# The last preparation ahead of the block products of Up, and the last gate's steps behind them, in another order

## The chip, the cores and the metric

The kernel runs on one core of a Trainium2 chip. The metric is the device time of one execution in microseconds (us), lower is better. Three runs of the kernel before gave 693.24, 691.15 and 691.52 us; the median is 691.52.

Engines are named as in the profile: PE is TensorE's matrix multiplication, PEld its loading of weights, DVE is VectorE, ACT ScalarE, POOL GpSimd, SP SyncE, which issues most DMAs (SPq is its queue). Each engine works off its own instructions in the order in which they are written; engines wait for one another by semaphores.

## The reference

One layer of a decoder, batch 1, 512 positions, width 1024, in f32. The change lies in its second half:

```python
mod = cs @ w_ada[l] + b_ada[l]                     # cs = silu(c)
sh1, sc1, gt1, sh2, sc2, gt2 = [m[:, None, :] for m in jnp.split(mod, 6, axis=-1)]
...
h2 = rmsnorm(x, norm2_g[l]) * (1.0 + sc2) + sh2
u = causal_dwconv(h2 @ w_up[l], conv_w[l], conv_b[l])   # w_up: 1024 x 5632, taps of width 3
a, v = jnp.split(u, 2, axis=-1)                         # 2816 columns each
x = x + gt2 * ((jax.nn.silu(a) * v) @ w_down[l])
```

What comes ahead of it (the projection, linear recurrence and sparse attention) is not touched.

## The kernel before

Every f32 operand of a matrix product is split into a high part (a cast by ScalarE, L150) and a low part (source minus high part, by VectorE, L151). `mm3` makes three matmuls of each product: high times high (L154), high times low (L155), low times high (L156). In the rows the parts of weights are called `whi`, `wlo` (or `wg` for both, in another pool), those of `h2` `h2h`, `h2l`. Thus weights must be loaded, cast and subtracted before the third matmul that uses them; for a down tile, where weights are the moving side's partner, `whi` serves the first and `wlo` the second matmul.

The Up product is computed in transposed form, 128 columns of `w_up` by 512 positions a tile. There are 44 such column blocks, and they run in this order:

- Sixteen plain tiles, `up_mm(st, ...)`, of 24 matmuls of 512 columns each: st 0 to 7 (`HEAD`, four column blocks of `a` and the same four of `v`) ahead, and st 8 to 15 (`BODY`) behind.
- Between them seven groups, `x_group(n)`, `n` from 0 to 6. A group makes the four column blocks `j`, `j+11` of `a` and of `v`: two by plain products (`v_mm`, weights `v1` and `v2`), two by a 2x2 block product with fewer multiplications, in which sums of weight blocks meet sums of blocks of `h2`. Sums of weights are three VectorE operations, `prepare_sums` (`t` or `t12` from `raw`); `prepare_plain` splits the blocks `b`, `prepare_rest` makes `t4` and splits the blocks `c`, `prepare_other` splits `v1`; within the group follow the splits of `t12`, of `x4` and of `v2`. Group `n` prepares group `n+1`; group 0 is prepared in the last tiles of the head. The sums of `h2` are made by POOL (`ar`, L1911 and the lines ahead of it) and split, one a tile, by `x_sum` in st 3 to 6 (rows `sx`).

Behind each tile come its `taps` (one ACT and two DVE operations, rows `y`) and its `gate` (Silu on ACT for `a`; three or four POOL operations, rows `ga` and `gb`, for `v`). They are written two tiles behind the tile. What is still open when the groups begin is held in a list and called at three places in a group.

Beside these runs the last gate, `gt2`: it is a matrix product with one row only, so `w_ada`'s slice is scaled by ScalarE and added up by POOL. `last_begin` clears `gt2` (a POOL memset), loads the row of `b_ada` and the first piece; `last_fetch` loads a piece (`aw`), `last_add` scales and adds one and fetches the next, sixteen in all, eight for each half `q`. `last_end(gt2, q)` splits the sum of a half into `rhi` and `rlo`, adds it up over the partitions by two matmuls with a matrix of ones (`ps<-rhi,onesr`, `ps<-rlo,onesr`: the spread), and copies `ps` back to `gt2`.

Loads of weights stand in a fixed list, `loads`; `take` issues them two or three ahead into `raw`, of two buffers; each third load of the groups goes into a lent buffer, `aw`, of one. A further chain of DMAs, `weight_sums(tick)`, sums blocks of `w_down` in memory, by SP (plain copies) and POOL (accumulating DMAs); `put_by` stores parts of the gated tiles in memory and splits others (rows `as`). Behind st 15 begins the down product (`dn`), whose weights come by `dn_load(u)` and are split by `dn_split(u)`.

Of the kernel before, what the change touches and what calls it, by code (L numbers as in the profile page):

```python
# [9 lines left out]
F32 = mybir.dt.float32  # L10
# [9 lines left out]
P = 128  # L20
# [89 lines left out]
def hybrid_layer_kernel(ctx: ExitStack, tc: tile.TileContext, d: dict, out: bass.AP, dbg=None):  # L110
# [14 lines left out]
    def nm(s):  # L125
        uid[0] += 1
        return f"{s}_{uid[0]}"
# [82 lines left out]

    loads += [up_load(f) for f in HEAD]
    first_x = len(loads)
    loads += [x_load(j, h) for j in XS for h in range(2)]
    last_x = len(loads)
# [3 lines left out]
    def issue():  # L218
        if len(issued) < len(loads):
            name, shape, pieces = loads[len(issued)]  # L220
            n = len(issued) - first_x
            if 0 <= n < 2 * len(XS) and n % 3 == 0:
                raw = wp.tile([P] + shape, F32, tag="aw", name=nm("raw"), bufs=1)
            else:
                raw = wp.tile([P] + shape, F32, tag="raw", name=nm("raw"))
            for sl, src in pieces:
                sp.dma_start(raw[sl], src)
            issued.append(raw)
# [1283 lines left out]

    def last_end(res, q):
        assert not last_raw
        acc = res[:, q * 512:(q + 1) * 512]
        hi, lo = (TMP([P, 512], F32R, tag=t) for t in ("rhi", "rlo"))
        split(hi, lo, acc)
        ps = PS()
        pe.matmul(ps, onesr, hi, start=True, stop=False)
        pe.matmul(ps, onesr, lo, start=False, stop=True)  # L1520
        sc.copy(acc, ps)

# [193 lines left out]
    us = {}  # L1716
# [53 lines left out]
    def gate(s, f):  # L1770
# [14 lines left out]
        else:  # L1785
# [3 lines left out]
            gp.tensor_tensor(a[:, 3], a[:, 0], b[:, 3], ALU.subtract)  # L1789

    def up_post(st):
        f, s = NF[st // 2], st % 2
        taps(us.pop(st), s, f)
        gate(s, f)

# [29 lines left out]
    def dn_load(u):  # L1825
        ph, v = divmod(u, NU)
        j = PAIRS[v]
        if u < 2:
            t = wp.tile([P, 2, 2, 512], F32, tag="raw", name=nm("raw"))
            r0, r1 = t[:, 0], t[:, 1]  # L1830
        else:
            r0, r1 = (G([2, 512], s="wd") for _ in range(2))
# [72 lines left out]
    up_mm(2, hi_half)  # L1905
    up_post(0)
    A = {(r, q): araw.pop((q, r)) for r in range(2) for q in range(2)}
    gp.tensor_tensor(A[1, 1], A[1, 0], A[1, 1], ALU.subtract)
# [65 lines left out]
    def x_group(n):  # L1974
# [14 lines left out]
        v_mm(V[0], p["v1"], range(4))  # L1989
        held.pop(0)()  # L1990
        beside()
        x_mm(X, half(p["t12"], 1), ops[2], False)
# [28 lines left out]
        if more:  # L2021
            prepare_other(n + 1)
        else:
            piece()
        del prep[n]

# [21 lines left out]
    for st in range(3, NH):  # L2048
        beside()
        up_mm(st, full)  # L2050
        up_post(st - 2)
        x_sum()
        if st == 3:
            last_begin(5, gt2)
        else:
            last_add(5, gt2)
        if st == NH - 3:
            prepare_sums(0)
        elif st == NH - 2:
            prepare_plain(0)  # L2060
        elif st == NH - 1:
            prepare_other(0)
            prepare_rest(0)
    held += [lambda: up_post(NH - 2), lambda: up_post(NH - 1), lambda: None]
    for n in range(len(XS)):
        x_group(n)
    SX.clear()
    for st in range(NH, nst):
        beside()
        if st == nst - 1:  # L2070
            dn_load(0)
            dn_load(1)
        up_mm(st, full)
        if held:
            for f in held:
                f()
            held.clear()
        elif st > NH + 1:
            up_post(st - 2)
        if st < NH + 5:  # L2080
            last_add(5, gt2)
        elif st < NH + 7:
            last_end(gt2, st - NH - 5)
    dn_split(0)
# [141 lines left out]
```

## Time and profile before

| | |
|---|---|
| median of 3 runs | 691.52 us |
| the profiled execution | 696.19 us, span 694.4 us |
| mean granted clock of TensorE | 0.988 |
| PE busy | 669.5 us, 96% of the span, 4400 matmuls |
| DVE, ACT, POOL busy | 552.9, 382.8, 180.7 us |
| st 3 begins | 343.21 us |
| group 0, group 1 begin | 373.51, 403.48 us |
| st 8 begins | 530.68 us |
| first down tile begins | 583.03 us |

Times within the execution count from the start of its span. In a row of the timeline stand the start, the duration, the engine, the line, the operation, what is written and read (`out<-in`), the shapes, and in brackets how long the engine stood idle just before and what released it.

### The profile page before, as it was taken

The page shows a single profiled execution, that of the slowest core. Times are in us where ns is not written, and L with a number is a line of the kernel's source. Part 1 is how long each engine was busy: PE and PEld are TensorE (multiplying, and loading weights), DVE is VectorE, ACT ScalarE, POOL GpSimd, SP SyncE. Part 2 cuts the span into 40 slices and gives each one's busy share as a digit, 9 for nine tenths or more (in the row PEclk, how much of TensorE's full clock was granted, in tenths as well). Part 3 has the DMA queues.
Part 4 walks back from the last instruction along what each step waited for, and adds up shares of the span by engine and source line. Part 5 has one row for each costly group of instructions (what it writes and reads, how often), then busy time and mean ns, then how long its engine had stood idle before and what let it go on. Part 6 is the DMA issues. An engine that isn't in the chain of part 4 may idle for free.

```text
span 694.4 us, 11710 instructions
## 1 busy us (share of the span) xinstructions
PE 669.5 (96%) x4400; PEld 562.1 (81%) x4400; DVE 552.9 (80%) x1038; ACT 382.8 (55%) x713; POOL 180.7 (26%) x172
## 2 busy tenths in 40 slices
PE   8999999999999999999997899999999988999996
PEld 4678898688888888888985798898988766888885
DVE  4788988978899878788568578988886877676997
ACT  4756437747777875346554454554554645465551
POOL 1006120000010101100656235664445864100000
PEclk9999999999999999999999899999999999999999
DMA  8936364566214135145356899999997736786672
GB/s 335 405 128 201 96 219 125 194 194 209 92 33 155 60 120 184 62 129 182 118 165 184 227 238 244 255 281 266 265 234 197 213 93 217 271 347 243 201 286 91
DMA packets 101885, 134.67 MB, mean 194 GB/s; under 512 B 6507, under 2 KB 67780, under 8 KB 101829
## 3 DMA queue, kind: packets, MB, share of 16 engines
q1 hardware_dynamic: 96885, 121.28, 51.5%
q0 software_dynamic: 4512, 11.54, 9.9%
q10 hardware_dynamic: 432, 1.12, 0.4%
q8 instruction: 34, 0.56, 0.3%
q14 instruction: 22, 0.18, 0.1%
HBM read 125.39 MB, written 31.60 MB: 226 GB/s over the span
## 4 chain that ended last, share of the span: by engine, by line
PE 69%; DVE 15%; ACT 7%; issue 3%; DMA 3%; POOL 1%; SPq 0%; ACTq 0%; DVEq 0%; POOLq 0%
PE u L154 5%; PE u L155 5%; PE u L156 5%; PE dn L155 5%; PE dn L156 5%; PE dn L154 5%; DVE wlo L151 4%; PE uf L156 4%; PE uf L155 3%; PE uf L154 3%; PE accq L679 3%; PE oh L154 2%; PE oh L156 2%; PE oh L155 2%; PE oT L1148 2%
## 5 line engine op out<-in xcount | busy, mean ns | idle before, releaser
L151 DVE TENSOR_TENSOR wlo<-raw,whi 128x1024 fp32r<-128x1024 f32 (+1 forms) x53 | 68.4, 1293 | 40.4 <-ACT whi L150 40.3
L156 PE MATMUL u<-h2h,wlo 128*128 128x512 f32 (+1 forms) x248 | 94.2, 380 | 3.1 <-DVE wlo L151 3.1
L154 PE MATMUL u<-h2h,whi 128*128 128x512 f32 (+1 forms) x248 | 94.4, 380 | 0.0
L155 PE MATMUL u<-h2l,whi 128*128 128x512 f32 (+1 forms) x248 | 94.0, 379 | 0.0
L150 ACT CAST whi<-raw 128x1024 fp32r<-128x1024 f32 (+1 forms) x53 | 53.9, 1018 | 17.3 <-PE u L155 6.9
L156 PEld LDWEIGHTS u<-h2h,wlo 128*128 128x128 f32 x248 | 47.0, 190 | 13.9 <-DVE wlo L151 5.2
L155 PEld LDWEIGHTS u<-h2l,whi 128*128 128x128 f32 x248 | 47.3, 191 | 7.9
L154 PEld LDWEIGHTS u<-h2h,whi 128*128 128x128 f32 x248 | 47.3, 191 | 7.7
L150 ACT CAST whi<-wd 128x1024 fp32r<-128x1024 f32 x20 | 21.1, 1055 | 39.8 <-PE dn L156 34.4
L371 POOL TENSOR_TENSOR hrs<-hrs,mhalf 128x4 f32<-128x4 f32 (+2 forms) x16 | 18.6, 1174 | 90.7 <-DVE hrs L370 88.6
L1086 ACT ACTIVATE pt<-pt,mx 128x128 f32<-128x128 f32 (+3 forms) x64 | 36.0, 564 | 9.2 <-DVE mx L1070 8.1
L154 PE MATMUL pT<-hT,whi 128*128 128x512 f32 x96 | 38.3, 399 | 0.0
L151 DVE TENSOR_TENSOR wlo<-wd,whi 128x1024 fp32r<-128x1024 f32 x20 | 25.5, 1275 | 15.4 <-ACT whi L150 15.3
L155 PE MATMUL pT<-hT,whi 128*128 128x512 f32 x96 | 37.6, 391 | 0.0
L156 PE MATMUL pT<-hT,wlo 128*128 128x512 f32 x96 | 37.5, 391 | 0.0
L155 PE MATMUL dn<-wlo,as 128*128 128x512 f32 x88 | 34.3, 390 | 0.1
L156 PE MATMUL dn<-whi,as 128*128 128x512 f32 x88 | 34.2, 389 | 0.0
L154 PE MATMUL dn<-whi,as 128*128 128x512 f32 x88 | 34.2, 389 | 0.0
L1126 ACT COPY pT<-F 128x512 f32<-128x512 f32 (+2 forms) x52 | 25.8, 499 | 13.5 <-PE F L1119 13.4
L1787 POOL TENSOR_TENSOR ga<-y,y 128x256 f32<-128x256 f32 x11 | 13.7, 1244 | 73.7 <-ACT y L1773 58.9
L1070 DVE CUSTOM_DVE_ANT_0 pt<-S,cmask 128x128 f32<-128x128 f32 (+3 forms) x64 | 29.7, 485 | 2.2 <-PE S L1066 2.0
L1773 ACT ACTIVATE y<-y 128x512 f32<-128x512 f32 x22 | 13.9, 633 | 30.8 <-DVE y L1767 30.8
(409 smaller groups left out, 2046.3 us busy)
## 6 DMA issues: line engine op xcount, KB each, us to landing
raw<-in_w_up SPq DMA_DIRECT2D x44, 512.0 KB, 6.8
aw<-in_w_ada SPq DMA_DIRECT2D x24, 512.0 KB, 3.9
ada<-in_ada_first SPq DMA_DIRECT2D x16, 512.0 KB, 7.9
raw<-in_w_in SPq DMA_DIRECT2D x7, 1024.0 KB, 5.5
wt<-in_w_down POOLq DMA_DIRECT2D x11, 512.0 KB, 9.0
wd<-in_w_down SPq DMA_DIRECT2D x11, 512.0 KB, 4.3
wt<-in_w_down SPq DMA_DIRECT2D x10, 512.0 KB, 5.2
wt<-in_w_down POOLq DMA_DIRECT2D x5, 1024.0 KB, 11.1
```

The lines of the kernel that those rows point to most:

```text
L150: sc.copy(hi, src)
L151: (eng or ve).tensor_tensor(lo, src, f32(hi), ALU.subtract)
L154: pe.matmul(o, ah, bh, start=start, stop=False, skip_group_check=True)
L155: pe.matmul(o, ah, bl, start=False, stop=False, skip_group_check=True)
L156: pe.matmul(o, al, bh, start=False, stop=stop, skip_group_check=True)
L371: gp.tensor_tensor(o, o, mhalf[:, 0:n], ALU.pow)
L679: pe.matmul(accq[i], h[:, e, i * P:(i + 1) * P], w[:, f], start=(k + e + f == 0), stop=(e == 1 and k == KT - 1), skip_group_check=True)
L1070: ve.tensor_tensor_reduce(pt[:, e * W:(e + 1) * W], ps[:, e * W:(e + 1) * W], cmask[:, 512 - W:512], -1.0, 1e30, ALU.add, ALU.min, mx[:, e ...
L1086: sc.activation(pt[:, sl], pt[:, sl], AF.Exp, bias=mx[:, e:e + 1], scale=-1.0, accum_out=su[:, h % 2, e:e + 1])
L1126: sc.copy(pT, ps[:, 0:n * P])
L1148: pe.matmul(oTs[i][r:r + 64, h // 2], VV[:, j, b, g], src[:, q * P:(q + 1) * P], start=(h == 0 and b == 0 and j == 0), stop=False, skip_gr ...
L1773: sc.activation(y, y, AF.Silu)
```

## The change

Five things are written elsewhere; no operation is added or left out.

1. The first load of group 0 (`ux2`) stands ahead of the head's last weight load and goes into the lent buffer; every third of the groups' loads after it does, as before.
2. Group 0's preparation is spread over st 4 to 7: sums, plain, rest, other. Before, the sums stood at st 5, plain at st 6, other and rest at st 7. In st 3 to 7 the taps come first, then `x_sum` and the preparation, then the gate.
3. `last_begin` stands ahead of POOL's four sums of `h2`. There is no `last_add` in st 4 to 7; groups 5 and 6 have a second one, st 8 has two, and st 9 to 13 one each.
4. `last_end` is cut in two. `last_split` of the first half stands at st 9 and `last_spread` at st 10; those of the second half at st 14 and st 15.
5. `dn_load(0)` stands at st 13, into the lent buffer, in place of st 15.

```diff
-    loads += [up_load(f) for f in HEAD]
+    x_loads = [x_load(j, h) for j in XS for h in range(2)]
+    loads += [*[up_load(f) for f in HEAD[:-1]], x_loads[0], up_load(HEAD[-1])]
     first_x = len(loads)
-    loads += [x_load(j, h) for j in XS for h in range(2)]
+    loads += x_loads[1:]
+    lent = {id(x) for x in x_loads[::3]}
...
-    def last_end(res, q):
+    def last_split(res, q):
         hi, lo = (TMP([P, 512], F32R, tag=t) for t in ("rhi", "rlo"))
-        split(hi, lo, acc)
+        split(hi, lo, res[:, q * 512:(q + 1) * 512])
+        last_parts.extend((hi, lo))
+
+    def last_spread(res, q):
         ps = PS()
-        pe.matmul(ps, onesr, hi, start=True, stop=False)
-        pe.matmul(ps, onesr, lo, start=False, stop=True)
-        sc.copy(acc, ps)
+        for n in range(2):
+            pe.matmul(ps, onesr, last_parts.pop(0), start=(n == 0), stop=(n == 1))
+        sc.copy(res[:, q * 512:(q + 1) * 512], ps)
...
-            t = wp.tile([P, 2, 2, 512], F32, tag="raw", name=nm("raw"))
+            t = wp.tile([P, 2, 2, 512], F32, tag=("raw" if u else "aw"), name=nm("raw"), bufs=2 if u else 1)
...
     up_post(0)
+    last_begin(5, gt2)
     A = {(r, q): araw.pop((q, r)) for r in range(2) for q in range(2)}
...
+        if n > 4:
+            last_add(5, gt2)
         beside()
...
             piece()
+            last_fetch(5)
...
     for st in range(3, NH):
         beside()
         up_mm(st, full)
-        up_post(st - 2)
+        post_taps(st - 2)
         x_sum()
-        if st == 3:
-            last_begin(5, gt2)
-        else:
-            last_add(5, gt2)
-        if st == NH - 3:
+        if st == NH - 4:
             prepare_sums(0)
-        elif st == NH - 2:
+        elif st == NH - 3:
             prepare_plain(0)
+        elif st == NH - 2:
+            prepare_rest(0)
         elif st == NH - 1:
             prepare_other(0)
-            prepare_rest(0)
-    held += [lambda: up_post(NH - 2), lambda: up_post(NH - 1), lambda: None]
+        post_gate(st - 2)
+
+    def between():
+        post_gate(NH - 2)
+        post_taps(NH - 1)
+
+    held += [lambda: post_taps(NH - 2), between, lambda: post_gate(NH - 1)]
...
     for st in range(NH, nst):
         beside()
-        if st == nst - 1:
+        if st == nst - 3:
             dn_load(0)
+        elif st == nst - 1:
             dn_load(1)
         up_mm(st, full)
...
-        if st < NH + 5:
+        for _ in range(2 if st == NH else st < NH + 6):
             last_add(5, gt2)
-        elif st < NH + 7:
-            last_end(gt2, st - NH - 5)
+        if st in (NH + 2, nst - 1):
+            last_spread(gt2, st == nst - 1)
+        if st in (NH + 1, nst - 2):
+            last_split(gt2, st == nst - 2)
     dn_split(0)
```

What this does to the engines' queues shows at three places. The first is VectorE's queue from st 4 to the last preparation ahead of group 0. Numbers behind names tell buffers apart; `wlo_792` before and `wlo_793` now are the low part of st 6's weights, `wlo_802` and `wlo_801` of st 7's, `t12_799` and `t12_789` the first group's sums. Before:

```order
L151 TENSOR_TENSOR sx_787_4345<-ar_754_4026,sx_786_4344 128x1024
L151 TENSOR_TENSOR wlo_792_4358<-raw_773_4262,whi_791_4357 128x1024
L1766 SCALAR_TENSOR_TENSOR y_793_4385<-u_772_4261,cv_3498,y_793_4385 128x511
L1767 SCALAR_TENSOR_TENSOR y_793_4385<-u_772_4261,cv_3498,y_793_4385 128x510
L151 TENSOR_TENSOR sx_795_4394<-ar_727_3879,sx_794_4393 128x1024
L1943 TENSOR_TENSOR t12_799_4407<-raw_790_4354 128x512
L1944 TENSOR_TENSOR raw_790_4354<-raw_790_4354 128x512
L1945 TENSOR_TENSOR t12_799_4407<-raw_790_4354 128x512
L151 TENSOR_TENSOR wlo_802_4413<-raw_773_4262,whi_801_4412 128x1024
L1766 SCALAR_TENSOR_TENSOR y_803_4440<-u_782_4310,cv_3498,y_803_4440 128x511
L1767 SCALAR_TENSOR_TENSOR y_803_4440<-u_782_4310,cv_3498,y_803_4440 128x510
L151 TENSOR_TENSOR sx_805_4446<-ar_728_3880,sx_804_4445 128x1024
```

Now:

```order
L151 TENSOR_TENSOR sx_787_4344<-ar_754_4026,sx_786_4343 128x1024
L1954 TENSOR_TENSOR t12_789_4350<-raw_774_4266 128x512
L1955 TENSOR_TENSOR raw_774_4266<-raw_774_4266 128x512
L1956 TENSOR_TENSOR t12_789_4350<-raw_774_4266 128x512
L151 TENSOR_TENSOR wlo_793_4361<-raw_788_4347,whi_792_4360 128x1024
L1771 SCALAR_TENSOR_TENSOR y_794_4388<-u_773_4265,cv_3498,y_794_4388 128x511
L1772 SCALAR_TENSOR_TENSOR y_794_4388<-u_773_4265,cv_3498,y_794_4388 128x510
L151 TENSOR_TENSOR sx_796_4393<-ar_727_3879,sx_795_4392 128x1024
L151 TENSOR_TENSOR wg_798_4397<-raw_774_4266,wg_797_4396 128x1024
L151 TENSOR_TENSOR wlo_801_4406<-raw_788_4347,whi_800_4405 128x1024
L1771 SCALAR_TENSOR_TENSOR y_802_4433<-u_782_4310,cv_3498,y_802_4433 128x511
L1772 SCALAR_TENSOR_TENSOR y_802_4433<-u_782_4310,cv_3498,y_802_4433 128x510
```

The three sums stand ahead of st 6's low part in place of behind it, and the first split of the group (`wg`) ahead of st 7's.

The second is SyncE's queue from `last_begin` and the first loads of `wt0` on (`raw<-in_w_up` are weights of Up, `gt2<-in_b_ada` the row of `last_begin`, `aw` pieces of the gate, `wt0` the sums of `w_down` in memory). Before:

```order
L1737 DMA wt0_3798<-in_w_down 128x2x512
L1738 DMA wt0_3798<-in_w_down 128x2x512
L227 DMA raw_773_4262<-in_w_up 128x8x128 x2
L1503 DMA gt2_3810<-in_b_ada 1x1024
L1498 DMA aw_781_4308<-in_w_ada 128x512
L1498 DMA aw_788_4350<-in_w_ada 128x512
L227 DMA raw_790_4354<-in_w_up 128x8x128 x2
L1498 DMA aw_796_4399<-in_w_ada 128x512
L227 DMA raw_797_4401<-in_w_up 128x8x128 x2
L227 DMA raw_798_4404<-in_w_up 128x8x128 x2
L1498 DMA aw_806_4451<-in_w_ada 128x512
L1742 DMA wt0_3798<-wt0_3798 128x2x512
```

Now:

```order
L1504 DMA gt2_3810<-in_b_ada 1x1024
L1499 DMA aw_772_4257<-in_w_ada 128x512
L1742 DMA wt0_3798<-in_w_down 128x2x512
L1743 DMA wt0_3798<-in_w_down 128x2x512
L228 DMA raw_774_4266<-in_w_up 128x8x128 x2
L228 DMA raw_788_4347<-in_w_up 128x8x128 x2
L228 DMA raw_791_4357<-in_w_up 128x8x128 x2
L1747 DMA wt0_3798<-wt0_3798 128x2x512
L228 DMA raw_810_4478<-in_w_up 128x8x128 x2
```

The row of `b_ada` and one piece stand ahead of `wt0`'s loads; the other pieces are gone from here, and the copy `wt0<-wt0` stood behind four weight loads and stands behind three, ahead of the fourth (`raw_798` before, `raw_810` now, the first for group 1).

The third is ScalarE's queue from st 15 into the down product (`gt2<-ps` copies a spread half, `whi_1082` and `wg_1084` are the high parts of the first down tile). Before:

```order
L1765 ACTIVATE y_1072_6318<-u_1054_6199,cv_3498 128x512
L1773 ACTIVATE y_1072_6318<-y_1072_6318 128x512
L150 CAST rhi_1073_6323<-gt2_3810 128x512
L1521 COPY gt2_3810<-ps_1075_6327 128x512
L1765 ACTIVATE y_1079_6365<-u_1060_6240,cv_3498 128x512
L150 CAST whi_1082_6374<-raw_1076_6332 128x1024
L150 CAST wg_1084_6378<-raw_1076_6332 128x1024
L1765 ACTIVATE y_1086_6382<-u_1069_6289,cv_3498 128x512
```

Now:

```order
L1770 ACTIVATE y_1073_6322<-u_1057_6205,cv_3498 128x512
L1778 ACTIVATE y_1073_6322<-y_1073_6322 128x512
L150 CAST rhi_1074_6327<-gt2_3810 128x512
L1770 ACTIVATE y_1078_6361<-u_1064_6250,cv_3498 128x512
L1526 COPY gt2_3810<-ps_1081_6370 128x512
L150 CAST whi_1082_6374<-raw_1063_6246 128x1024
L150 CAST wg_1084_6378<-raw_1063_6246 128x1024
L1770 ACTIVATE y_1086_6382<-u_1070_6293,cv_3498 128x512
```

The copy of the second half stood ahead of the taps of tile 13 and of the down tile's casts; it now stands behind these taps, directly ahead of the casts. On TensorE the two matmuls that it waits for stood behind st 14's, and now stand behind st 15's.

More of the change, by code (lines that the diff above doesn't have):

```diff
@@ L220, in issue @@
             name, shape, pieces = loads[len(issued)]
-            n = len(issued) - first_x
-            if 0 <= n < 2 * len(XS) and n % 3 == 0:
+            if id(loads[len(issued)]) in lent:
                 raw = wp.tile([P] + shape, F32, tag="aw", name=nm("raw"), bufs=1)
@@ L1511, in last_add @@
         last_fetch(s)
-    def last_end(res, q):
-        assert not last_raw
-        acc = res[:, q * 512:(q + 1) * 512]
+    last_parts = []
+    def last_split(res, q):
+        assert all(raw[1] > q for raw in last_raw)
         hi, lo = (TMP([P, 512], F32R, tag=t) for t in ("rhi", "rlo"))
-        split(hi, lo, acc)
+        split(hi, lo, res[:, q * 512:(q + 1) * 512])
+        last_parts.extend((hi, lo))
+    def last_spread(res, q):
         ps = PS()
-        pe.matmul(ps, onesr, hi, start=True, stop=False)
-        pe.matmul(ps, onesr, lo, start=False, stop=True)
-        sc.copy(acc, ps)
+        for n in range(2):
+            pe.matmul(ps, onesr, last_parts.pop(0), start=(n == 0), stop=(n == 1))
+        sc.copy(res[:, q * 512:(q + 1) * 512], ps)
     x1 = []
@@ L1789, in gate, with post_taps, post_gate @@
             gp.tensor_tensor(a[:, 3], a[:, 0], b[:, 3], ALU.subtract)
+    def post_taps(st):
+        taps(us.pop(st), st % 2, NF[st // 2])
+    def post_gate(st):
+        gate(st % 2, NF[st // 2])
     def up_post(st):
-        f, s = NF[st // 2], st % 2
-        taps(us.pop(st), s, f)
-        gate(s, f)
+        post_taps(st)
+        post_gate(st)
     tick = [2]
@@ L2050, in hybrid_layer_kernel @@
         up_mm(st, full)
-        up_post(st - 2)
+        post_taps(st - 2)
         x_sum()
-        if st == 3:
-            last_begin(5, gt2)
-        else:
-            last_add(5, gt2)
-        if st == NH - 3:
+        if st == NH - 4:
             prepare_sums(0)
+        elif st == NH - 3:
+            prepare_plain(0)
         elif st == NH - 2:
-            prepare_plain(0)
+            prepare_rest(0)
         elif st == NH - 1:
             prepare_other(0)
-            prepare_rest(0)
-    held += [lambda: up_post(NH - 2), lambda: up_post(NH - 1), lambda: None]
+        post_gate(st - 2)
[3 more added lines that the diff above has]
+    held += [lambda: post_taps(NH - 2), between, lambda: post_gate(NH - 1)]
     for n in range(len(XS)):
```

## The prediction

> **What bounds the kernel now.** I read the page first, then TensorE's part of the timeline for every idle time from 338 to 590 us, and last the rows of the engines named there as releasers.
>
> ```profile
> span 694.4 us, 11710 instructions
> ...
> PE 669.5 (96%) x4400; PEld 562.1 (81%) x4400; DVE 552.9 (80%) x1038; ACT 382.8 (55%) x713; POOL 180.7 (26%) x172
> ...
> PEclk9999999999999999999999899999999999999999
> ```
>
> TensorE is busy 96% of the span, so only time in which it waits, or runs slowly after a wait, can be won. The clock dips once, in slice 23 (382 to 399 us). The sum goes against the profiled run: 696.19 us, of which 694.4 are span. It lies 4.67 us above the median of 691.52, so I subtract from both alike. The next rows are TensorE's, from the start of st 3 to the start of group 2; the bracket is the idle time ahead and what ended it.
>
> ```profile
> 343.21 0.40 PE L154 MATMUL u<-h2h,whi 128*128 128x512 f32 x1
> ...
> 354.12 0.39 PE L154 MATMUL u<-h2h,whi 128*128 128x512 f32 x1
> ...
> 368.37 0.50 PE L156 MATMUL u<-h2h,wlo 128*128 128x512 f32 x1 [2.49 <-DVE wlo L151]
> ...
> 374.98 0.39 PE L156 MATMUL uf<-h2h,wg 128*128 128x256 f32 x1 [1.07 <-DVE wg L151]
> ...
> 384.85 0.58 PE L154 MATMUL uf<-sx,whi 128*128 128x256 f32 x1 [3.90 <-ACT m L1988]
> ...
> 385.83 0.58 PE L156 MATMUL uf<-sx,wlo 128*128 128x256 f32 x1 [0.20 <-DVE wlo L151]
> ...
> 403.48 0.28 PE L154 MATMUL uf<-h2h,wg 128*128 128x256 f32 x1
> ...
> 424.50 0.28 PE L154 MATMUL uf<-h2h,wg 128*128 128x256 f32 x1
> ```
>
> St 3 and st 4 take 354.12-343.21 = 10.91, so an undisturbed tile is 5.455 us; group 1 takes 424.50-403.48 = 21.02. From the start of st 3 to the start of group 1, five tiles and a group would take 5x5.455+21.02 = 48.3; they take 60.27. The head thus loses 12.0 us: 2.49+1.07+3.90+0.20 = 7.66 in idle time, and 4.3 in slow matmuls. These two rows group one kind of matmul by form, in 376.5 to 391 us (group 0) and in 391 to 412 us, and the third is the table by stretch (busy time of PE, PEld, DVE, ACT, POOL, then the granted clock).
>
> ```profile
> L155 PE MATMUL uf<-sx,whi 128*128 128x256 f32 x8 | 3.3, 415 | 0.0
> ...
> L155 PE MATMUL uf<-sx,whi 128*128 128x256 f32 x8 | 2.3, 283 | 0.0
> ...
> 380.00:390.00 10.00, 5.91 (x26) 5.10 (x25) 5.19 (x6) 2.89 (x5) 4.74 (x5) 0.72 0.76 243
> ```
>
> Behind the 3.90 us of idle time the granted clock is 0.72 and a matmul takes 415 ns in place of 283. Between group 1 and st 8 TensorE shows no wait worth counting. The end of Up, st 8 to the first down tile:
>
> ```profile
> 530.68 0.40 PE L154 MATMUL u<-h2h,whi 128*128 128x512 f32 x1
> ...
> 553.96 0.50 PE L156 MATMUL u<-h2h,wlo 128*128 128x512 f32 x1 [0.26 <-DVE wlo L151]
> ...
> 566.70 0.50 PE L1520 MATMUL ps<-rlo,onesr 128*128 128x512 f32 x1 [1.76 <-DVE rlo L151]
> ...
> 574.93 0.49 PE L1519 MATMUL ps<-rhi,onesr 128*128 128x512 f32 x1 [2.22 <-ACT rhi L150]
> ...
> 575.65 0.80 PE L1520 MATMUL ps<-rlo,onesr 128*128 128x512 f32 x1 [0.23 <-DVE rlo L151]
> ...
> 583.03 0.39 PE L154 MATMUL dn<-whi,as 128*128 128x512 f32 x1
> ```
>
> ```profile
> 570.00:580.00 10.00, 7.55 (x25) 5.57 (x25) 6.48 (x8) 5.05 (x8) 2.42 (x3) 0.83 0.74 222
> ```
>
> Eight tiles and four spread matmuls at a 24th of a tile would take 8x5.455+4x0.227 = 44.5; they take 52.35. The tail loses 7.8: 4.5 in these idle times, most of it at the two spreads, and 3.3 in slow matmuls and smaller waits, with a clock of 0.83 behind the second spread.
>
> **The change part by part.** It removes and adds no arithmetic: the same casts, subtractions, adds and loads stand in another order. Worth is only which wait goes and which comes.
>
> *The head.* TensorE waits there for VectorE's queue, and that for others:
>
> ```profile
> 351.66 0.75 DVE L1767 SCALAR_TENSOR_TENSOR y<-u,cv,y 128x510 f32<-128x510 f32 x1
> ...
> 353.31 0.26 SPq L1503 DMA_DIRECT2D gt<-in_b_ada  x1
> 354.11 1.23 DVE L151 TENSOR_TENSOR sx<-ar,sx 128x1024 fp32r<-128x1024 f32 x1 [1.70 <-ACT sx L150]
> 354.54 0.42 SPq L227 DMA_DIRECT2D raw<-in_w_up  x1
> ...
> 356.87 0.72 ACT L1509 ACTIVATE aw<-aw,cs 128x512 f32<-128x512 f32 x1 [2.79 <-DMA aw<-in_w_ada]
> ...
> 358.57 1.53 DVE L151 TENSOR_TENSOR wlo<-raw,whi 128x1024 fp32r<-128x1024 f32 x1 [3.23 <-ACT whi L150]
> ...
> 362.59 1.77 DVE L1943 TENSOR_TENSOR t<-raw 128x512 f32<-128x512 f32 x1
> ...
> 365.55 1.11 DVE L1945 TENSOR_TENSOR t<-raw 128x512 f32<-128x512 f32 x1
> 366.58 1.74 DVE L151 TENSOR_TENSOR wlo<-raw,whi 128x1024 fp32r<-128x1024 f32 x1
> ...
> 393.43 0.68 DVE L1943 TENSOR_TENSOR t<-raw 128x512 f32<-128x512 f32 x1
> ```
>
> SyncE stands until 353.31 at the load of `b_ada`, which waits for the late memset. The load of `aw` behind it comes late, ScalarE stands until 356.87 at scaling it, the cast of st 6's weights stands behind that, and VectorE is idle from 355.34 to 358.57. The first group's weights are issued at 354.54, so their sums (three steps, 362.59 to 366.66) come late and stand ahead of the low part of st 7's weights (366.58), for which TensorE waits 2.49; the rest of group 0's preparation is late behind them, up to the 3.90.
>
> Now the memset and `b_ada` stand four POOL operations earlier, the adds of st 4 to 7 are gone from ScalarE's and POOL's queues, group 0's weights are loaded a tile's load ahead, and the sums come at st 4. I lay VectorE's new order on its own durations. `sx` at 352.4, behind the tap that ends at 352.41 (ScalarE casts it ahead of the Silu now, so 1.7 sooner than 354.11); the sums behind it to 355.7 with three times 0.68, or to 357.6 with 1.77+1.11+1.11; st 6's low part at 356.7 to 359.0, where TensorE uses it at 360.0 (start of st 6, 354.12+5.455, and two matmuls). From there, with two taps at 0.75, `sx` 1.23, low parts of 1.22 to 1.77 and `t4` like a step of the sums, the low part of st 7 is done at 362.9 to 365.2 (use at 365.5). Group 0 would start at 343.21+5x5.455 = 370.5; `v1` is used some 3.3 and `t12` 5.8 us into it: `v1` is done at 370.7 to 374.0 (use at 373.8), `t12` at 373.7 to 376.8 (use at 376.3). Every wait goes, with at most 0.5 left at the slow ends, and with the 3.90 the slow clock. Bounds: 12.0 if all goes, 0 if VectorE is no sooner than before; I take 11.5, near the upper, because only the last two uses are touched by the slow ends, and because POOL, beside whose work the sums were slow, is emptied of its adds just there.
>
> The gates of st 1 to 5 move behind the preparation: POOL's work, none of which TensorE waits for here; cover is POOL's idle time. The load into the lent buffer is the same DMA, issued sooner. The two adds put into groups 5 and 6 are ScalarE's (a scale of 0.72, as at 356.87) and POOL's, which are busy 55% and 26% of the span: nothing, under TensorE's 21 us of a group.
>
> *The tail.* The rows behind the end of Up and those that come to matter:
>
> ```profile
> 551.59 2.31 DVE L151 TENSOR_TENSOR wlo<-raw,whi 128x1024 fp32r<-128x1024 f32 x1
> ...
> 576.48 0.59 ACT L1521 COPY gt<-ps 128x512 f32<-128x512 f32 x1 [1.61 <-PE ps L1520]
> 577.64 1.04 ACT L150 CAST whi<-raw 128x1024 fp32r<-128x1024 f32 x1
> 579.23 1.22 DVE L151 TENSOR_TENSOR wlo<-raw,whi 128x1024 fp32r<-128x1024 f32 x1
> 580.36 1.77 DVE L151 TENSOR_TENSOR wg<-raw,wg 128x1024 fp32r<-128x1024 f32 x1
> ...
> 586.45 1.22 DVE L151 TENSOR_TENSOR wlo<-raw,whi 128x1024 fp32r<-128x1024 f32 x1
> ```
>
> Both spreads stand a tile behind their splits now, so the idle times at 566.70, 574.93 and 575.65 (4.2) go and the slow clock behind them with them; if nothing came instead, all 7.8. What comes:
> First, st 8 takes two adds and its neighbours the split of the first half. The subtraction of st 12's low part, done at 553.90 before and used on the spot (TensorE waited 0.26), stands behind the extra copy of the gate half on ScalarE (0.59) and behind VectorE's split; I put it at 555.2, a wait of 1.4.
> Second, the copy of the second half (0.59, as at 576.48) waits for the spread behind st 15, and `whi` of the first down tile stands behind it in ScalarE's queue. With 7.8-1.4 = 6.4 us won, st 15 and its spread end about 583.03-6.4 = 576.6, and the spread's last matmul leaves at 576.9; copy to 577.5, `whi` (1.04) to 578.5, where it was done at 578.68 under cover of st 15. So the first down tile waits 1.8, and its second matmul for `wlo` (1.22) another 1.2.
> Third, from there VectorE and ScalarE go through the same chain as before: `wlo`, `wg` (1.77), two taps (1.5), Silu, cast, taps (1.5), `wlo` of down tile 1 (1.22). It ended at 586.45+1.22 = 587.67; from a copy about 0.4 later than before (576.9 against 576.48), with taps already done, I get 587.3. Before, down tile 1 started at 583.03+5.455 = 588.5 and had its parts; now it waits for them and starts in effect at 587.5.
> So of 6.4 us won by st 15, 1.0 is left at down tile 1. Bounds: 6.4 if ScalarE's and VectorE's chain came sooner than I lay it, -1 if TensorE's new waits slow the clock through two down tiles. I take 1.0, the value that the chain's own rows give.
>
> A wait as short as 2.22 us (574.93) was followed by a clock of 0.83 and slow matmuls, while the page's slice with the 2.49 of 368.37 (365 to 382 us) still shows 9. [...]
>
> Sum: 11.5+1.0 = 12.5. Span 681.9, run 683.7, median 679.0.
>
> **The rivals.** *The head's wait goes by half* (12%): VectorE's work up to group 0 is unchanged, and only its idle 3.2 us before 358.57 come forward. Of 7.66 idle some 4.5 stays at `v1` and `t12`, in waits too short for the slow clock: won 12.0-4.5 = 7.5 in the head and nothing in the tail, where I count on 1.0; median 684.0. For it: the slow ends of my times stand at the uses. If the short waits slow the clock as the 2.22 did, up to 3.3 less is won; by the row of 2.49 nothing less.
> *The tail's waits vanish too* (14%): if ScalarE's casts of the first down tile are out before its use, all 6.4 stays: 11.5+6.4 = 17.9, median 673.6. Against it: the copy stands ahead of `whi` in one queue.
> *The tail turns worse* (12%): the waits of 1.8 and 1.2 follow upon each other, and the clock drops for two down tiles as behind 574.93, 2x3.3 of which 2.3 lie beside the chain: 4.3 lost, median 683.3. For it: the clock of 0.83 behind a shorter wait.
> *No change* (5%): if the order in which the queues run doesn't free VectorE, because the groups' own preparation takes the debt over (VectorE, at 80% of the span, has some 4 us free in a group of 21) and pays it at group 1 or 2; median 691. Against it: 4 us in each of seven groups pays off the whole.
>
> One on the other side: *SyncE is blocked by a copy* (5%).
>
> ```profile
> 358.96 1.41 POOL L1740 DMA_DIRECT2D wt<-in_w_down  x1
> ...
> 371.72 0.56 SPq L1742 DMA_DIRECT2D wt<-wt  x1
> ```
>
> ```profile
> raw<-in_w_up SPq DMA_DIRECT2D x44, 512.0 KB, 6.8
> ```
>
> The copy `wt<-wt` waits for POOL's accumulating DMA, issued 12.8 us before it, and now stands ahead of the weights of group 1. VectorE's sums want those 10.05 us ahead of that group (393.43 against 403.48), now at 391.5-10 = 381.5; with 6.8 to land, the copy decides from 375 on. POOL's DMA no longer waits behind an add and would come near 352.5, the copy near 365. Only a copy beyond 375+12.5 = 387.5 would eat all that is won; at 390 the median is 694.
>
> **How the numbers follow.** My forecast has 52%. Faster by over 0.3% (2.07 us, about what a measurement of this kernel can tell from no change) are the forecast and the first three rivals, 90%; the same 5%, slower 5%. The range runs from 673.5 (both stalls gone) to 684.5 (head by half, or tail worse); the last two stay out, with some of the ends, about 2 in 10.
>
> **What would show it.** Right: no wait of TensorE between st 6 and the end of group 0, group 1's start at 391.5, the granted clock 1.0 from 370 to 400; the spread matmuls without idle time; a wait of about 1.4 in st 12, then of 1.8 at `whi` and 1.2 at `wlo` of the first down tile, then of 1 to 2 at down tile 1. Wrong: waits for `v1` or `t12` in group 0, a late SyncE row ahead of group 1's weights, or no wait at all at the first down tile.

## The result and the profile after

The changed kernel takes 682.04 us (median of 4 runs, 680.94 to 683.32), the kernel before 691.70 on the same chip (4 runs). The ratio is 0.9858, 95% interval 0.9832 to 0.9883: 9.7 us faster. On a second chip it was 682.75 against 692.63, 0.9855 (0.9832 to 0.9878).

The page of the changed kernel:

```profile
span 679.2 us, 11713 instructions
...
PE 662.6 (98%) x4400; PEld 557.9 (82%) x4400; DVE 549.6 (81%) x1038; ACT 382.7 (56%) x713; POOL 179.4 (26%) x172
...
PEclk9999999999999999999999999999999999999999
```

The span is 15.2 us shorter, though the medians differ by 9.7 only; why is in the part on the prediction. TensorE's timeline, with every wait from st 3 to the down product:

```profile
340.92 0.40 PE L154 MATMUL u<-h2h,whi 128*128 128x512 f32 x1
...
368.15 0.28 PE L154 MATMUL uf<-h2h,wg 128*128 128x256 f32 x1
...
389.16 0.28 PE L154 MATMUL uf<-h2h,wg 128*128 128x256 f32 x1
...
516.38 0.40 PE L154 MATMUL u<-h2h,whi 128*128 128x512 f32 x1
517.32 0.50 PE L156 MATMUL u<-h2h,wlo 128*128 128x512 f32 x1 [0.32 <-DVE wlo L151]
...
541.29 0.50 PE L156 MATMUL u<-h2h,wlo 128*128 128x512 f32 x1 [1.16 <-DVE wlo L151]
...
564.99 0.49 PE L154 MATMUL dn<-whi,as 128*128 128x512 f32 x1 [1.62 <-ACT whi L150]
...
566.62 0.50 PE L155 MATMUL dn<-wlo,as 128*128 128x512 f32 x1 [1.14 <-DVE wlo L151]
...
572.26 0.47 PE L154 MATMUL dn<-wg,as 128*128 128x512 f32 x1 [0.81 <-DVE y L1772]
...
578.65 0.39 PE L154 MATMUL dn<-whi,as 128*128 128x512 f32 x1
```

St 3 to group 1 takes 389.16-340.92 = 48.24 us in place of 60.27, with no wait in it at all. Group 1 to st 8 takes 127.2, as before. From st 8 on, the waits at the spreads are gone and four others have come: 1.16 in st 12, 1.62 and 1.14 at the parts of the first down tile, and 0.81 in its second half, for a tap. That one is not for data: by the program, the taps of st 15 are the last to read a bank of the accumulators that the down product takes over. The third down tile begins 578.65-516.38 = 62.27 us behind st 8, where it was 593.91-530.68 = 63.23. SyncE's copy `wt<-wt` ran at 360.31 and held nothing up.

Next come the row of the table by stretch for 380 to 390 us, where the granted clock was 0.72 before and is 1.00 now, and VectorE's rows of the head:

```profile
380.00:390.00 10.00, 10.00 (x64) 9.05 (x63) 9.81 (x15) 6.47 (x9) 3.57 (x3) 1.00 0.68 194
```

```profile
351.17 0.69 DVE L1954 TENSOR_TENSOR t<-raw 128x512 f32<-128x512 f32 x1
...
353.23 1.22 DVE L151 TENSOR_TENSOR wlo<-raw,whi 128x1024 fp32r<-128x1024 f32 x1
...
359.18 1.75 DVE L151 TENSOR_TENSOR wlo<-raw,whi 128x1024 fp32r<-128x1024 f32 x1
...
366.62 1.22 DVE L151 TENSOR_TENSOR wlo<-raw,whi 128x1024 fp32r<-128x1024 f32 x1
...
369.21 1.23 DVE L151 TENSOR_TENSOR wlo<-t,whi 128x1024 fp32r<-128x1024 f32 x1
```

The sums run from 351.17 on, the low parts of st 6 and st 7 are done at 354.45 and 360.93, `v1` at 367.84 and `t12` at 370.44. Group 0 begins at 368.15 and its first matmuls with the low parts of `v1` and `t12` start at 371.49 and 374.00, 3.3 and 5.9 us into it: about 3.6 us to spare at each.

### The profile page after: what moved, and what is told of

The parts are those of the page before. It is cut to its first block, busy times and chain, and to the rows that moved or that the text cites. A ratio compares the mean times of both kernels' runs of the same rounds, so it can differ in the third digit from the quotient of the medians.

```text
span 679.2 us, 11713 instructions
## 1 busy us (share of the span) xinstructions
PE 662.6 (98%) x4400; PEld 557.9 (82%) x4400; DVE 549.6 (81%) x1038; ACT 382.7 (56%) x713; POOL 179.4 (26%) x172
## 5 line engine op out<-in xcount | busy, mean ns | idle before, releaser
L151 DVE TENSOR_TENSOR wlo<-wd,whi 128x1024 fp32r<-128x1024 f32 x20 | 25.5, 1276 | 15.2 <-ACT whi L150 15.2
L1511 POOL TENSOR_TENSOR gt<-gt,aw 128x512 f32<-128x512 f32 x16 | 23.8, 1486 | 21.8 <-ACT aw L1510 21.5
```

The lines of the kernel that those rows point to most:

```text
L151: (eng or ve).tensor_tensor(lo, src, f32(hi), ALU.subtract)
L1511: gp.tensor_tensor(acc, acc, r, ALU.add)
```

## The experiments

The stages of all traces, in us, worked out from the rows as above ("to third down tile" is the start of the third one, from st 8):

| kernel | st 3 begins | st 3 to group 1 | st 8 to third down tile | ratio to before on the same chip |
|---|---|---|---|---|
| before | 343.21 | 60.27 | 63.23 | 1 |
| before, three more traces | 343.21, 340.73, 341.23 | 59.85, 61.14, 60.15 | 63.11, 63.14, 62.04 | |
| changed | 340.92 | 48.24 | 62.27 | 0.9858 |
| changed, two more traces | 340.20, 341.11 | 48.24, 48.24 | 62.23, 62.64 | 0.9855 |
| head only | 342.57 | 48.24 | 64.43 | 0.9868 |
| tail only | 341.84 | 60.07 | 60.65 | 0.9980 |
| copy behind | 341.61 | 48.24 | 60.46 | 0.9819 |
| order only | 341.19 | 48.24 | 60.65 | 0.9812 |
| relief only | 342.99 | 53.56 | 62.64 | 0.9918 |
| copy and taps | 341.60 | 48.23 | 60.34 | 0.9800 |
| order, copy and taps | 342.41 | 48.24 | 57.67 | 0.9760 |

Where an expectation says "the fifth down tile", it means the start of this third one. Each ratio is to the kernel before on the same chip; brackets hold its 95% interval.

**The kernel before, again.**

> The kernel before, unchanged, run again to see how its executions differ. The two profiles shown differ by 15.2 us in span, the medians only by 9.7. Theory A (slow clock varies): TensorE's idle times stand in every execution of the kernel before (2.5, 1.1 and 3.9 in the head, 1.8 and 2.2 at the spreads), while the slow matmuls behind them (4.3 in the head, about 3 in the tail) come in some executions only; the new profile then has the same idle times to 0.3 us each, but st 3 to group 1 takes 56 to 58 us in place of 60.3, or the tail 49 to 50 in place of 52.4, and runs of about 691 us show a mean granted clock of 0.992 or more. Theory B (the start varies): head and tail take 60.3 and 52.4 us again within 0.5, and the difference lies ahead of 343 us, where the profile of before has a clock of 0.83 between 10 and 20 us.

Its waits in the head and its start:

```profile
368.00 0.50 PE L156 MATMUL u<-h2h,wlo 128*128 128x512 f32 x1 [2.38 <-DVE wlo L151]
...
374.60 0.39 PE L156 MATMUL uf<-h2h,wg 128*128 128x256 f32 x1 [1.07 <-DVE wg L151]
...
384.54 0.58 PE L154 MATMUL uf<-sx,whi 128*128 128x256 f32 x1 [3.91 <-ACT m L1988]
```

```profile
10.00:20.00 10.00, 9.06 (x63) 5.26 (x63) 6.22 (x18) 5.90 (x17) 1.32 (x3) 0.83 1.03 412
...
380.00:390.00 10.00, 5.90 (x26) 5.16 (x25) 4.88 (x6) 2.89 (x5) 4.70 (x4) 0.69 0.77 247
```

Ratio 1.0011 (0.9991 to 1.0031). Head (59.85) and tail (63.11) are as in the first trace, slow matmuls and all, and so is the low clock at the start. This execution (695.91 us) was as slow as the first, so it can't say where a faster one gains; the shorter head that theory A expected did not show.

**The head's part alone.** As the changed kernel, but with both steps of a half together and the loads as before:

```diff
-        if st == nst - 3:
+        if st == nst - 1:
             dn_load(0)
-        elif st == nst - 1:
             dn_load(1)
...
+        if st in (NH + 5, NH + 6):
+            last_split(gt2, st == NH + 6)
+            last_spread(gt2, st == NH + 6)
```

> Only the head's part of the change (order of loads, preparation over four tiles, early memset and no adds in st 4 to 7; the adds as in the changed kernel), with both steps of each gate half together at st 13 and 14 and the down loads at st 15 as before. My theory: st 3 to group 1 takes 48.3 us as in the changed kernel, and the waits at the two spreads are back (1.8 and 2.2 or more, as the last add now ends a tile later); median 0.5 to 2.5 us over the changed kernel, 682.5 to 684.5. Rival (the tail's part carries much of the gain, because the slow clock behind the second spread is worth 3): 685 to 687.

```profile
542.46 0.50 PE L156 MATMUL u<-h2h,wlo 128*128 128x512 f32 x1 [1.16 <-DVE wlo L151]
...
555.20 0.50 PE L1525 MATMUL ps<-rlo,onesr 128*128 128x512 f32 x1 [1.51 <-DVE rlo L151]
...
563.42 0.50 PE L1525 MATMUL ps<-rhi,onesr 128*128 128x512 f32 x1 [2.26 <-ACT rhi L150]
```

682.96 us, 0.9868 (0.9846 to 0.9890), inside my range. The head is the changed kernel's; the waits at the two spreads are back (1.51 and 2.26), and st 12 waits 1.16 here too, without the early copy and split of the first half. So these two did not make that wait.

**The tail's part alone.** The old head, adds and loads; the new places of split, spread and `dn_load(0)`:

```diff
-        for _ in range(2 if st == NH else st < NH + 6):
+        for _ in range(st < NH + 5):
             last_add(5, gt2)
```

> Only the tail's part of the change (split of each gate half a tile or more ahead of its spread, first down load at st 13), head and adds as before, without second adds. My theory: the waits at the spreads go, the wait for whi (1.6) and wlo (1.1) of the first down tile and the 0.8 behind it come, and 0 to 1.5 us are won: median 690 to 692. Rival: 3 to 4 us are won because the slow clock behind the second spread goes too: 687.5 to 688.5.

```profile
552.78 0.50 PE L156 MATMUL u<-h2h,wlo 128*128 128x512 f32 x1 [0.19 <-DVE wlo L151]
...
576.47 0.49 PE L154 MATMUL dn<-whi,as 128*128 128x512 f32 x1 [1.62 <-ACT whi L150]
...
577.73 0.50 PE L155 MATMUL dn<-wlo,as 128*128 128x512 f32 x1 [0.77 <-DVE wlo L151]
```

691.30 us, 0.9980 (0.9963 to 0.9996): 1.4 us won by the ratio and 1.8 by the medians, 1.5 at most by my theory. In the trace it wins 63.11-60.65 = 2.5, more than the 1.0 of the full change. St 12 waits 0.19 and `wlo` 0.77, where the changed kernel has 1.16 and 1.14: what differs in this stretch is only the adds.

**The copy behind the casts.**

```diff
     dn_split(0)
+    last_copy()          # the sc.copy of the second half's ps
     up_post(nst - 2)
```

> The changed kernel with one line moved: the copy of the second gate half out of its spread stands behind the casts of the first down tile on ScalarE, not ahead of them. My theory (the down tile waits because its casts stand behind a copy that waits for TensorE): whi is cast under st 15, the waits of 1.62 and 1.14 fall to under 0.5 in all, the one of 0.81 behind them grows to 1.2 to 1.4, and the down product begins its second tile 2.3 us earlier against st 8: median about 679.8. Rival (the casts wait for the weights or their buffers, not for the copy): no change of the waits, median within 0.7 of the changed kernel's.

```profile
564.99 0.50 PE L155 MATMUL dn<-wlo,as 128*128 128x512 f32 x1 [0.72 <-DVE wlo L151]
...
571.16 0.47 PE L154 MATMUL dn<-wg,as 128*128 128x512 f32 x1 [1.33 <-DVE y L1779]
```

680.07 us, 0.9819 (0.9796 to 0.9843). The wait for `whi` is gone, the one for `wlo` falls to 0.72, the one for the bank grows to 1.33: in all 2.05 in place of 3.57, and the third down tile comes 1.8 us sooner. The copy in ScalarE's queue was what the down tile waited for; of the expected 2.3 us, 0.5 is missing, with a wait of 0.72 left at `wlo` where I expected less than 0.5.

**The changed kernel on the second chip.**

> The changed kernel, unchanged, on one chip with the kernel before and three variants. On the first chip it won 9.7 us of median (0.9832 to 0.9883), where the two profiles differ by 13.2 from the start of st 3 on. Theory A: what is won in every execution is the idle time (7.7 in the head, 4.5 at the spreads, less the 4.7 of new waits, so 7.5 to 8), and the slow matmuls behind it in part of the executions (1 to 4 us more on the mean, a granted clock that rises from 0.991 to about 0.995): 9.5 to 11.5 under the kernel before on the same chip, and the profile has the waits of 1.2, 1.6, 1.1 and 0.8 again. Theory B (slow matmuls are lost in every execution of before): 12.5 to 13.5 under it.

682.75 against 692.63, 9.9 won, with the same waits (1.15, 1.62, 1.09, 0.80). The time fits theory A, but no trace of before has the shorter head that was its reason.

**Only the order.** Memset, `b_ada` and the adds back in st 3 to 7, none added later:

```diff
-    last_begin(5, gt2)
...
         x_sum()
+        if st == 3:
+            last_begin(5, gt2)
+        else:
+            last_add(5, gt2)
```

> The changed kernel with memset, the load of b_ada and the adds of st 4 to 7 back where they stood before, and none added in the groups or doubled at st 8: of the head's part only the order of preparation and of the weight loads is left. My theory (VectorE is late because the sums and splits stand too late in its own queue): two thirds or more of the head's 12 us stay won, with a wait of 0.5 to 3 for st 7's weights or for v1, since ScalarE still stands about 3 us at the scaled piece; median 1 to 4 over the changed kernel. Rival (VectorE is late because it stands idle behind ScalarE and SyncE): less than half is won, 6 or more over the changed kernel.

```profile
343.52 0.96 POOL L1503 MEMSET gt<- 128x1024 f32 x1
...
372.77 1.22 DVE L151 TENSOR_TENSOR wlo<-t,whi 128x1024 fp32r<-128x1024 f32 x1
...
540.37 0.50 PE L156 MATMUL u<-h2h,wlo 128*128 128x512 f32 x1 [0.19 <-DVE wlo L151]
...
547.50 1.30 POOL L1511 TENSOR_TENSOR gt<-gt,aw 128x512 f32<-128x512 f32 x1 [0.27 <-ACT aw L1510]
...
564.06 0.49 PE L154 MATMUL dn<-whi,as 128*128 128x512 f32 x1 [1.62 <-ACT whi L150]
...
565.32 0.50 PE L155 MATMUL dn<-wlo,as 128*128 128x512 f32 x1 [0.77 <-DVE wlo L151]
```

The sixteenth add (547.50 here) in the changed kernel:

```profile
558.94 1.29 POOL L1511 TENSOR_TENSOR gt<-gt,aw 128x512 f32<-128x512 f32 x1
```

679.99 us, 0.9812 (0.9791 to 0.9834): 2.8 us under the changed kernel on the same chip, where I expected 1 to 4 over it. The traces give 1.6 of this (60.65 against 62.23); the rest goes with higher clocks (0.995 to 0.999 here, 0.992 to 0.995 in four of the other's five). All of the head's 12 us is there. VectorE finishes `t12` at 373.99, 5.57 us into group 0, which begins at 368.42, and TensorE uses it at 374.27: 0.3 us to spare, against 3.6 in the changed kernel. That spare time is what taking the adds out of st 4 to 7 buys; TensorE has no use for it. And with the adds back, st 12 waits 0.19 and `wlo` 0.77, as with the tail alone: the sixteenth add ends 32.1 us behind the start of st 8, in the changed kernel 43.9.

One part of the relief stays here: since the gates stand behind `last_begin` now, the memset runs at 343.52, 2.3 us behind the start of st 3, where it ran at 352.32, 9.1 us behind it, in the kernel before. So the load of `b_ada`, which SyncE issued at 353.31 in the kernel before, right behind the memset's end (352.32+0.96), should come some 7 us sooner against st 3 and hold SyncE less; that is an estimate from these rows. No run has the new order with the memset as late as before, so whether the order wins the head without this is not shown, and the rival, VectorE idle behind SyncE and ScalarE, is excluded only as far as the adds go.

**Only the relief.** The old order and loads in the head, with early memset and no adds in st 4 to 7:

```diff
-        if st == NH - 4:
+        if st == NH - 3:
             prepare_sums(0)
...
         elif st == NH - 1:
             prepare_other(0)
+            prepare_rest(0)
```

> The changed kernel with the head's preparation and its weight loads in the old order (sums at st 5, plain at st 6, other and rest at st 7), but memset and b_ada early and no adds in st 4 to 7. My theory: VectorE's idle 3.2 us and the slow sums go, so the wait of 2.5 in st 7 goes, and a wait of 2 to 4.5 in group 0 stays, for t12 or what hangs on it: median 3 to 6 over the changed kernel. Rival: the relief alone wins the whole head, within 1 of it.

```profile
377.48 1.03 ACT L150 CAST whi<-t 128x1024 fp32r<-128x1024 f32 x1
378.42 0.36 ACT L1999 COPY m<-uf 128x256 f32<-128x256 f32 x1
...
378.83 0.39 PE L154 MATMUL uf<-sx,whi 128*128 128x256 f32 x1 [2.84 <-ACT m L1999]
```

```profile
380.00:390.00 10.00, 10.00 (x60) 9.49 (x61) 5.47 (x8) 3.93 (x6) 4.58 (x5) 0.83 0.75 193
```

687.07 us, 0.9918 (0.9899 to 0.9937), 4.3 over the changed kernel, as expected: the head takes 53.56, with a wait of 2.84 for the copy of `m`, which stands behind the late cast of `t` on ScalarE, and a clock of 0.83 behind it. The gains do not add up: the relief alone wins 6.7 us of the head, the order with the earlier memset 12.0, all together 12.0.

**Copy and taps.**

```diff
-    up_post(nst - 2)
-    up_post(nst - 1)
+    post_taps(nst - 2)
+    post_taps(nst - 1)
+    post_gate(nst - 2)
+    post_gate(nst - 1)
```

> The kernel with the copy behind the first down tile's casts, and also the taps of st 15 ahead of the gate of st 14. The wait of 1.33 in the first down tile was put down to VectorE's last tap of st 15, on which a bank of the accumulators hangs; these taps stand behind ScalarE's Silu, which waits for VectorE's taps of st 14. My theory: that wait falls under 0.3, and the second down tile starts 1.0 to 1.4 us sooner against st 8 than with the copy alone moved: median about 1.1 less than its 0.9819 of before gives (679 where before is 693.1). Rival: the time comes back at the second down tile's low part, which stands behind the same taps: within 0.5 of it.

```profile
564.97 0.50 PE L155 MATMUL dn<-wlo,as 128*128 128x512 f32 x1 [0.67 <-DVE wlo L151]
...
572.05 0.50 PE L155 MATMUL dn<-wlo,as 128*128 128x512 f32 x1 [1.25 <-DVE wlo L151]
```

679.21 us, 0.9800 (0.9778 to 0.9822). The wait for the bank is gone, and 1.25 come back at the low part of the second down tile, which stands behind the same taps: 60.34 against 60.46. By the traces the rival was right. The ratio is 0.0019 lower than with the copy alone, 1.3 us, but the two intervals overlap; so the times can't tell the two apart.

**Order, copy and taps.** The order alone, with the copy behind both taps:

```diff
-    up_post(nst - 2)
-    up_post(nst - 1)
+    post_taps(nst - 2)
+    post_taps(nst - 1)
+    last_copy()
+    post_gate(nst - 2)
+    post_gate(nst - 1)
```

> The kernel with the order alone (adds of st 4 to 7 as before), and in it the copy of the second gate half behind the first down tile's casts and behind both last taps, which stand ahead of the gates. My theory: with the sixteenth add done four tiles sooner VectorE is free for the first down tile's low part before st 15 ends, so the waits of 1.62, 0.77 and 0.79 all go and none takes their place: st 8 to the fifth down tile takes 56 us in place of 60.65, median 4 to 5 under the order alone, 0.974 to 0.976 of before. Rival (TensorE waits for the low part of the second down tile as in the kernel with copy and taps moved, 1.25): 58 to 60 us, 0.978 to 0.980.

```profile
541.53 0.50 PE L156 MATMUL u<-h2h,wlo 128*128 128x512 f32 x1 [0.18 <-DVE wlo L151]
...
570.17 0.50 PE L155 MATMUL dn<-wlo,as 128*128 128x512 f32 x1 [0.89 <-DVE wlo L151]
```

676.47 us, 0.9760 (0.9736 to 0.9784), the fastest version: with the sixteenth add done sooner, the split of its sum starts 41.2 us behind st 8 (43.9 with copy and taps only, where it waits 1.33 for the add), the first down tile's low part is ready at 563.03, and TensorE passes from st 15 into that tile at 563.43 without a wait. Of the second tile's wait 0.89 is left, so the stretch takes 57.67, between mine (56) and the rival's (58 to 60).

**Two more profiles of the kernel before.**

> The kernel before, one more look for a profile. If the slow matmuls vary and the idle times do not: idle times of 2.4 to 2.5, 1.1, 3.9, 1.8 and 2.2 again; st 3 to group 1 between 56 and 60.3, the start (0 to 343 us) between 340 and 343.2, whichever the mean clock leaves.

> The same once more: one of the stretches with a low clock (10 to 20 us, 380 to 390 us, 570 to 580 us) should be absent in at least one of the two looks if the clock's loss depends on where an idle time falls, and all three present in both if each idle time costs its slow matmuls always.

The first of them:

```profile
365.54 0.69 PE L156 MATMUL u<-h2h,wlo 128*128 128x512 f32 x1 [2.39 <-DVE wlo L151]
...
376.24 0.50 PE L156 MATMUL u<-h2h,wlo 128*128 128x512 f32 x1 [0.46 <-DVE wlo L151]
...
383.26 0.58 PE L154 MATMUL uf<-sx,whi 128*128 128x256 f32 x1 [4.45 <-ACT m L1988]
```

```profile
10.00:20.00 10.00, 9.23 (x70) 5.55 (x69) 7.37 (x24) 7.00 (x21) 1.23 (x3) 1.00 1.03 414
...
360.00:370.00 10.00, 7.61 (x27) 5.77 (x27) 8.05 (x7) 2.98 (x4) 7.03 (x6) 0.83 1.05 247
...
570.00:580.00 10.00, 7.53 (x26) 5.54 (x25) 6.48 (x8) 4.97 (x7) 2.42 (x3) 0.83 0.91 291
```

The second, at the second spread:

```profile
572.78 0.50 PE L1519 MATMUL ps<-rhi,onesr 128*128 128x512 f32 x1 [0.60 <-ACT rhi L150]
```

```profile
560.00:570.00 10.00, 8.22 (x30) 6.27 (x29) 7.81 (x8) 5.06 (x7) 5.70 (x6) 0.83 0.25 94
...
570.00:580.00 10.00, 9.17 (x39) 7.02 (x38) 6.78 (x9) 4.97 (x7) 2.98 (x2) 1.00 0.95 292
```

694.5 and 693.05 us. The idle times moved a little: the 1.07 for `wg` became 0.42 to 0.46 for `v1`, and 3.90 became 4.45, so they do not stand still as one theory had it; their sum in the head stays between 7.5 and 7.7. At 10 to 20 us the clock is 1.00 in both, and st 3 begins 2.0 to 2.5 us sooner. Slow matmuls stand behind other waits than in the first trace (now also at 360 to 370 us), but the head takes 60.15 to 61.14 in all. Only in the second of these traces is the tail shorter, by 1.1: its slow stretch follows the first spread, which waits 1.78, and the second spread waits 0.60 in place of 2.2. Of the three stretches with a low clock in the first trace, the one at 10 to 20 us is absent in both, the one at 570 to 580 us in the second, the one at 380 to 390 us in neither (0.66 and 0.83).

**One more profile of the changed kernel.**

> The changed kernel, one more look for a profile: both of its profiles so far are of executions with a mean clock of 0.999, while most of its timed runs have 0.992 to 0.995 and take 2 us more. The idle times should be 1.2, 1.6, 1.1 and 0.8 again. If the clock of this execution is below 0.997, the stretch that lost it shows: by one theory the first down tile (560 to 580 us), slowed behind the new waits as the second spread was in the kernel before; by the other the start (10 to 20 us, st 3 at 342 to 343), which the change does not touch.

```profile
565.18 0.49 PE L154 MATMUL dn<-whi,as 128*128 128x512 f32 x1 [1.62 <-ACT whi L150]
566.82 0.50 PE L155 MATMUL dn<-wlo,as 128*128 128x512 f32 x1 [1.15 <-DVE wlo L151]
```

```profile
560.00:570.00 10.00, 7.24 (x26) 5.33 (x25) 6.33 (x7) 5.02 (x8) 3.32 (x5) 0.88 0.48 117
```

681.51 us at a mean clock of 0.995. The first down tile lost it: 0.88 in 560 to 570 us. It takes longer, and so the wait for the bank (0.81) doesn't arise; the third down tile comes only 0.4 us later than in the other two traces.

## Why the prediction was right, and where not

The forecast was 679.0 with 673.5 to 684.5; it is 682.04. The direction was right, and so was the mechanism of the head; in the tail the sum came out, but one of its waits had another cause. The gain of 12.5 was 9.7.

- *The head, 11.5.* It measured 12.0 (60.27 to 48.24), and 11.6 to 12.9 against the other traces of before: the upper bound. Group 1's start, forecast at 391.5 with st 3 at 343.21, stands 389.16 with st 3 at 340.92. With the 2.29 us by which st 3 differs added, the low parts of st 6 and st 7, `v1` and `t12` were done at 356.7, 363.2, 370.1 and 372.7: at the fast ends of the plan or ahead of them, with sums of 0.69.
- *Why I took 11.5.* One reason was that POOL is emptied of its adds. That was not needed: with the adds in place the new order wins the whole head too, with 0.3 us to spare at `t12`. Whether the earlier memset was needed stays open.
- *The tail, 1.0.* From st 8 to the third down tile 0.96 is won, and each of the new waits came: 1.16 (forecast 1.4), 1.62 (1.8), 1.14 (1.2), 0.81 (1 to 2). But two terms lay under that sum which I had not seen apart. The new places of split, spread and first down load win 2.5 (tail only), and the moved adds cost 1.6 of it (62.27 against 60.65 with the order only). The forecast had put the wait of st 12 down to the extra copy and the split; "head only" has it without these, and "tail only" lacks it with them. It is the adds, and that 1.4 came near 1.16 is luck. So is 1.2 against 1.14: the forecast left out that the first matmul covers part of the low part's 1.22 (0.77 is left with "order only", where it takes 1.23), and in the changed kernel the low part took 1.60. The forecast gave the adds a price only in the groups ("nothing, under TensorE's 21 us of a group"), where none shows, and none in st 8 to 13, where the sixteenth ends 12 us later.
- *The last wait.* I put it at the second down tile's low part, and it stood a few matmuls ahead, at an accumulator's bank that the last taps hold. With these taps moved ahead, the low part is what TensorE waits for next.
- *The slow clock at the first down tile.* The rival with the worse tail put it at 3.3 us a tile, from the row of 574.93, of which 2.3 lie beside the chain; the 2.3 was an estimate from the forecast's own times (the chain to 587.3, the tile alone to about 585, 576.6+1.8+1.2+5.455), and no run shows it. One trace of three has the slow clock: 0.88 in 560 to 570 us and 0.95 in 570 to 580, 1.2+0.5 = 1.7 us of clock, and 0.4 of it shows in the end. ("Relief only", with the same two waits, has it too: 0.83 at 570 to 580 us.)
- *The step that was mis-sized* is "I subtract from both alike". The profiled execution of before had a mean granted clock of 0.988, as low as any of the 58 others that have a clock on record (0.988 to 0.995, mean 0.991); the one of the changed kernel 0.999, the highest of ten (0.992 to 0.999, mean 0.9945). Of these 58, the executions at 0.988 took 694.6 on the mean (11 of them) and at 0.995 691.0 (5); of the changed kernel 683.0 at 0.992 (3) and 680.9 at 0.999 (2). The two traces thus stand some 15 us apart, 13 from st 3 on, and what is typical 10. At one and the same clock of 0.995 the two differ by 691.0-681.5 = 9.5. I took a gain out of an execution that had lost more than most. This does not close the sum: the 58 and the ten executions, taken over all chips, average 693.1 and 682.2, 10.9 apart, and the two traces nearest to these means (693.05 us at 0.991 and 681.51 at 0.995) stand 11.5 apart. What is left between 9.7 and these is inside the interval of the ratio (8.1 to 11.6 us).

Where the other executions gain or lose their clock is shown in part only. The start, which the change does not touch, shifts st 3 by up to 3 us (340.2 to 343.2); the tail of before varies by 1.2, the first down tile of the changed kernel by 0.4. The head of before took 59.9 to 61.1 in all five traces with its old order. No trace caught an execution of before under 693 us, so which of its stretches is shorter there stays open.

That slow matmuls come and go with the same wait ahead bears on two rows of the prediction, the 2.22 with a clock of 0.83 behind it and the 2.49 with none as low. Waits of 2.22 to 2.25 at the second spread were followed by 0.83 in three traces of before. Waits of 2.39 and 2.35 in st 7 were followed by a clock of 0.83 to 0.87 in two traces, while 2.49 and 2.38 in the first two traces were followed by 1.00; 1.62 and 1.15 by 0.88 in one of three. So in these runs the length of a wait of 1.6 to 2.5 us does not tell which clock follows it, and what does is not shown. That waits of 4.5 us in all at `v1` and `t12` would be too short for the slow clock, as the rival with half of the head had it, was the author's estimate. No run shows such a limit: the 1.76 at the first spread was followed by a clock of 1.00 in the first trace of before (570 to 574 us), the 1.78 there by 0.83 (560 to 570 us) in the last.

## What to carry to other kernels

Lay the waiting engine's new order on the durations of its own rows and compare each end with the place of its use; that gave the head and the first down tile's wait for `whi` to 0.5 and 0.2 us. Give a moved piece of side work its price where it lands, above all in a stretch where another engine already ends just in time: the adds taken out of the head bought 3.3 us that TensorE had no use for, and cost 1.6 in the tail. Before subtracting from a profiled execution, look at its mean clock against that of the timed runs: a gain in slow matmuls counts only as often as they occur.

## What was not expected of the hardware

Behind waits of 1.6 to 2.5 us the granted clock fell to 0.83 to 0.88 (mean of 10 us) in some executions and not in others of the same kernel. In steps of 2 us the fall has one shape: behind the second spread of the kernel before, 574 to 580 us have 0.90, 0.50 and 0.75, so 2x(0.10+0.50+0.25) = 1.7 us of clock are lost, and 564 to 570 us in the last trace of before have 0.87, 0.50 and 0.78, again 1.7. Behind the 3.90 in the first trace it is twice that (0.61, 0.50, 0.50 and 0.68 from 384 to 392 us). The time moves by up to 6 us between executions (690.1 to 696.0 for the kernel before) with mean clocks of 0.995 to 0.988. VectorE's operation on 128x512 took 0.69 us with POOL idle (363.43 in the changed kernel) and 1.77 beside POOL's products (362.59 in the kernel before). A low part of 128x1024 took 1.22 at most places and 2.31 at 551.59 in the kernel before, where POOL ran an add until 552.82.
